# Softmax scores and gated-attention products as pairs of 64-row matmuls, with matmul operands at multiples of 128 bytes

## The chip, the cores and the metric

The kernel runs on one core of one Trainium2 chip. The metric is device time in microseconds (us) of one execution, the median of several runs.

## The reference, cut to what matters

One decoder layer on x of 2048 tokens by 1024 channels, float32. The normed input is projected by w_in to the inputs of three branches; their outputs are joined, scaled, projected by w_out and added to x; then comes a gated MLP with a short causal convolution.

```python
proj = rms(x) @ w_in                       # (2048, 2064)
# gated linear attention, 4 heads, dk 32, dv 64, chunks of 64 tokens
attn = where(causal, einsum('nid,njd->nij', q_dec, k_inv), 0)    # per chunk and head
o = attn @ v + q_dec @ state_before                              # per chunk and head
# sliding-window attention, 8 query heads of 64 on 2 key/value heads, blocks of 128
scores = q @ k_window.T * 64**-0.5 + band_bias                   # (128, 256) per head and block
out = softmax_with_sink(scores) @ v_window
# causal convolution of width 31, layer norm, silu; then
x = x + concat(o_a, o_b, o_c) * branch_scale @ w_out
x = x + (silu(gate) * val) @ w_down
```

## The kernel before, in words

All 2048 tokens are handled in four chunks of 512 (`NCH`, `T`), each of four blocks of 128 (`NT`, `P`). The program has three stages. The attention stage, up to 858 us, holds norm, input projection (`in_proj`, the groups gA to gD), the three branches (`attention`) and the output projection (`out_proj`; the last chunk's falls into the next pools and its tile is again called op). The two FFN stages (the u tiles up to 1705 us, then the d tiles) follow.

Products of accuracy are done in three: an operand is split into a high and a low part of type float32r (`split`, `piece_split`), and `mm3` (lines 145 to 148) issues high by high (L146), high by low (L147) and low by high (L148). Plain float32 matmuls (ga, gd, go) show as two matmul instructions each, as they go in two passes.

Events carry positions written out by hand (`SCHED`), and are emitted in that order; the framework then orders the instructions of each engine anew, by when it takes their inputs to be ready and by emission, and gives out buffers as they come free. So matmuls of different events stand between each other on TensorE (PE). PSUM has eight banks: four of pool A (`bankA`, accumulators of the projections) and four of pool B (`bankB`), which all transposes and all products of the branches share, one bank a tile.

The scores of one block are in `s2` of `swa_steps` (lines 687 to 724). Four transposes put the normed q into PSUM, `split` writes it to `qT` (ScalarE, ACT, the high part; VectorE, DVE, the low part). For each of four head pairs j, `mm3` multiplies qT, whose partitions hold the 64 channels of two heads, by `kz`. kz holds the keys of each of the two key heads in its own half of the partitions and zeros in the other, so that one 128-row matmul of 512 columns gives the scores of both heads (256 keys each) in one bank. In the first block of all only 128 keys exist and the matmul has 256 columns. Two reductions (L707) then add the bias and take the maximum. `k_norm_b` writes kz, one half of the partitions at a time (L551 on ACT, L552 on DVE).

The gated attention's inner products are in `g1` (lines 595 to 608): `qbd` holds the decayed q of four heads block-diagonally (four ACT copies of 32 rows), one float32 matmul ga (L604) of 128 rows and 512 columns gives all four heads' products in one bank, and L607 on DVE copies them under a mask to `attn`. In `g2`, L617 multiplies the two 64-token halves of `kts` and `va`: two matmuls of 64 rows, on partitions 0 to 63 and 64 to 127, into two banks (gd and go).

Addresses, in bytes within a partition, follow from the pools in order, every tile rounded up to 32 bytes, behind 16384 bytes of DMA scratch:

| tile | first address | past a multiple of 128 |
|---|---|---|
| mix, hT (attention), hb (FFN) | 18560, 34944, 51328, 67712 | 0 |
| kz | 95424 | 64 |
| vp | 105664 | 64 |
| wz | 92320 | 32 |
| hl (split weights, attention stage) | 125888, then every 4096 | 64 |
| qT, pT | 213536, 217888 | 32 |
| hl, hu (from 812 us on, FFN) | 174208, then every 4096 | 0 |
| hg, hw (second FFN stage) | 98432, 114816, then every 4096 | 0 |

Of the kernel before, what the change touches and what calls it, by code (L numbers as in the profile page):

```python
# [21 lines left out]
T = 512  # L22
NT = T // P
NCH = S // T
EPS = 1e-6
NEG = -1e30
# [15 lines left out]
NPRE = 4  # L42
OLD, OLA = 4, 1.5
NSC = NCH // 2
KH = KD // 2
# [20 lines left out]
def f32(ap):  # L66
    return ap.bitcast(F32)
# [3 lines left out]
def hymba_layer(  # L71
# [50 lines left out]
    def bankB(n):  # L122
        return psB.tile([P, T], F32, tag="b", name=n)
# [186 lines left out]
    cst = cp.tile([P, N_CST], F32, name="cst")  # L310
    tails = cp.tile([P, NUP, 2], F32, name="tails")
    with ExitStack() as p1:
        c1 = p1.enter_context(tc.tile_pool(name="c1", bufs=1))
        bt = c1.tile([P, SH, 2 * BLK], F32, name="bt")
        negsink = c1.tile([P, SH], F32, name="negsink")
        wz = c1.tile([P, KD, 32], F32R, name="wz")
        wa2 = c1.tile([32, P], F32, name="wa2")
# [3 lines left out]

        kz = c1.tile([P, 2, 2, (NT + 1) * BLK], F32R, name="kz")
        vp = c1.tile([P, NT + 1, 2, 192], F32R, name="vp")
        attn_b = c1.tile([P, GH, P], F32, name="attn")
        qbd = c1.tile([P, GH, P], F32, name="qbd")
        st_b = [c1.tile([P, GH * GDV], F32, name=f"st{i}") for i in range(2)]
# [4 lines left out]
        xp = p1.enter_context(tc.tile_pool(name="xp", bufs=2))  # L331
        ip = p1.enter_context(tc.tile_pool(name="ip", bufs=1))
        resp = p1.enter_context(tc.tile_pool(name="resp", bufs=2))
        at = p1.enter_context(tc.tile_pool(name="at", bufs=1))

        def tmp(n):
# [10 lines left out]

        for b in [f32(kz), f32(vp), attn_b, qbd, halo] + st_b:
            dve.memset(b, 0.0)
# [183 lines left out]
        def k_norm_a(c, t, a):  # L533
            sq = at.tile([P, P], F32, tag="ksq", name=f"ksq{c}_{t}")
            st = at.tile([P, 4], F32, tag="kst", name=f"kst{c}_{t}", bufs=2)
            act.activation(out=sq, in_=a[:, 0:P], func=AF.Square)
            dve.tensor_reduce(out=st[:, 0:2], in_=sq.rearrange("p (s d) -> p s d", d=SHD), axis=AX.X, op=ALU.add)
            rstd_of(st[:, 2:4], st[:, 0:2], 2, 1.0 / SHD)
            av = a[:, 0:P].rearrange("p (s d) -> p s d", d=SHD)
            pool.tensor_tensor(out=av, in0=av, in1=st[:, 2:4].unsqueeze(2).broadcast_to([P, 2, SHD]), op=ALU.mult)  # L540

        def k_norm_b(c, t, a):
            if t == 0 and c > 0:
                dve.tensor_copy(kz[:, :, :, 0:BLK], f32(kz[:, :, :, NT * BLK:]))
# [12 lines left out]
            split(dH, dL, vv)  # L557

        def gla_gates(c, d):
# [16 lines left out]
            e2 = at.tile([P, T], F32, tag="e2", name=f"e2_{c}")  # L576
            dec = at.tile([P, T // GC], F32, tag="dec", name=f"dec_{c}")
            qk = d["qk"]
# [12 lines left out]
        def gla_steps(c, d, mix):  # L591
# [3 lines left out]
            def g1(t):  # L595
                qd, ki, kt, dec = d["g"]
                ts = slice(t * P, (t + 1) * P)
                ap = bankB(f"ga{c}_{t}")
                for h in range(GH):
                    hs = slice(h * GDK, (h + 1) * GDK)  # L600
                    act.copy(qbd[hs, h, :], qd[hs, ts])
                dp = bankB(f"gd{c}_{t}")
                pe.transpose(dp[:, 256:256 + P], kt[:, ts], ident)
                pe.matmul(ap, ki[:, ts], qbd.rearrange("p h i -> p (h i)"), start=True, stop=True)  # L604
                kts = at.tile([P, P], F32, tag="kts", name=f"kts{c}_{t}")
                act.copy(kts, dp[:, 256:256 + P])
                dve.copy_predicated(attn_b.rearrange("p h i -> p (h i)"), gmask.rearrange("p h i -> p (h i)"), ap)  # L607
                w[t].update(dp=dp, kts=kts)

            def g2(t):  # L610
# [21 lines left out]
                sq = at.tile([P, 256], F32, tag="osq", name=f"osq{c}_{t}")  # L632
                ss = at.tile([P, 8], F32, tag="oss", name=f"oss{c}_{t}", bufs=2)
                act.activation(out=sq, in_=op[:, 0:256], func=AF.Square)
# [24 lines left out]
        def q_norm(c, t, q):  # L659
            sq = at.tile([P, T], F32, tag="tmp", name=f"qsq{c}_{t}", bufs=NTMP)  # L660
            st = at.tile([P, 16], F32, tag="qst", name=f"qst{c}_{t}", bufs=2)
# [11 lines left out]
        def swa_steps(c, t, d, mix):  # L673
# [13 lines left out]
            def s2():  # L687
                tp = bankB(f"qtp{c}_{t}")
                for j in range(4):
                    pe.transpose(tp[:, j * P:(j + 1) * P], w["qn"][:, j * P:(j + 1) * P], ident)  # L690
                qT = at.tile([P, 2, T], F32R, tag="qT", name=f"qT{c}_{t}")
                split(qT[:, 0, :], qT[:, 1, :], tp)
# [3 lines left out]
                else:  # L696
                    s_sb = [at.tile([P, 4, 2 * BLK], F32, tag=f"s{s}", name=f"s{s}_{c}_{t}") for s in range(2)]
                st = at.tile([P, 4, SH], F32, tag="sst", name=f"sst{c}_{t}", bufs=2)
                for j in range(4):
                    sp_ = bankB(f"sc{c}_{t}_{j}")  # L700
                    so = sp_[:, 0:2 * wd]
                    js = slice(j * P, (j + 1) * P)
                    ks = slice(t * BLK + o0, (t + 2) * BLK)
                    mm3(so, qT[:, 0, js], qT[:, 1, js], kz[:, 0, :, ks], kz[:, 1, :, ks], True, True)
                    for s in range(2):
                        h = 2 * j + s
                        dve.tensor_tensor_reduce(out=s_sb[s][:, j, o0:], in0=sp_[:, s * wd:(s + 1) * wd],  # L707
                                                 in1=bt[:, h, o0:], scale=1.0, scalar=NEG,
                                                 op0=ALU.add, op1=ALU.max, accum_out=st[:, 0, h:h + 1])
                dve.scalar_tensor_tensor(out=st[:, 0, :], in0=st[:, 0, :], scalar=-1.0, in1=negsink,  # L710
# [14 lines left out]
            def s3t(i):  # L725
                s, kb = combos[i]
                tp = bankB(f"ptp{c}_{t}_{s}{kb}")
                for j in range(4):
                    pe.transpose(tp[:, j * P:(j + 1) * P], w["sv"][s][:, j, kb * BLK:(kb + 1) * BLK], ident)
                pT = at.tile([P, 2, T], F32R, tag="pT", name=f"pT{c}_{t}_{s}{kb}", bufs=2)  # L730
                split(pT[:, 0, :], pT[:, 1, :], tp)
                w[i] = pT
# [26 lines left out]
        def conv_steps(c, d):  # L759
# [15 lines left out]
            def c1_(t):  # L775
                ts = slice(t * P, (t + 1) * P)
                tp = bankB(f"cy{c}_{t}")
                for i in range(2):
                    pe.transpose(tp[:, i * P:(i + 1) * P], ys[i][:, ts], ident)
                bn = at.tile([P, 12], F32, tag="bn", name=f"bn{c}_{t}", bufs=2)  # L780
# [585 lines left out]
```

## Time and profile before

| | |
|---|---|
| median of 3 runs (lowest, highest) | 2141.02 us (2140.99, 2143.72) |
| the profiled execution | 2137.3 us |
| its span, first to last instruction | 2135.6 us |
| PE busy | 2076.2 us |
| DVE busy | 1703.3 us |
| ACT busy | 1187.8 us |
| mean granted clock of TensorE | 0.994 |

The span is what the profile's rows add up to; the profiled execution's own time is 1.7 us longer. Busy time of PE counts a matmul from its start to its modelled end, and neighbouring matmuls overlap, so the rate of a stream is read from the distance between starts. PEld is the loading of weights, which runs beside the matmuls.

### The profile page before, as it was taken

The page shows a single profiled execution, that of the slowest core. Times are in us where ns is not written, and L with a number is a line of the kernel's source. Part 1 is how long each engine was busy: PE and PEld are TensorE (multiplying, and loading weights), DVE is VectorE, ACT ScalarE, POOL GpSimd, SP SyncE. Part 2 cuts the span into 40 slices and gives each one's busy share as a digit, 9 for nine tenths or more (in the row PEclk, how much of TensorE's full clock was granted, in tenths as well). Part 3 has the DMA queues.
Part 4 walks back from the last instruction along what each step waited for, and adds up shares of the span by engine and source line. Part 5 has one row for each costly group of instructions (what it writes and reads, how often), then busy time and mean ns, then how long its engine had stood idle before and what let it go on. Part 6 is the DMA issues. An engine that isn't in the chain of part 4 may idle for free.

```text
span 2135.6 us, 27892 instructions
## 1 busy us (share of the span) xinstructions
PE 2076.2 (97%) x9296; PEld 1658.3 (78%) x9296; DVE 1703.3 (80%) x2898; ACT 1187.8 (56%) x2281; POOL 295.4 (14%) x400
## 2 busy tenths in 40 slices
PE   6999999999999999999999999999999999999999
PEld 5766777777777767888888888888888868888887
DVE  4987986798689777877888978787787789678965
ACT  5467656766686665665655545455454534444443
POOL 1132121221121210011000013222122000000000
PEclk9999999999999999999999999999999999999999
DMA  4222224342433217544444576222222295887262
GB/s 141 86 91 63 60 86 147 94 119 93 135 103 101 66 59 245 175 132 147 152 165 168 182 260 218 79 71 98 79 89 79 89 346 161 290 281 232 70 207 89
DMA packets 183923, 296.22 MB, mean 139 GB/s; under 512 B 18832, under 2 KB 98019, under 8 KB 183779
## 3 DMA queue, kind: packets, MB, share of 16 engines
q1 hardware_dynamic: 183779, 294.45, 42.1%
q8 instruction: 73, 1.20, 0.2%
q14 instruction: 71, 0.58, 0.1%
HBM read 231.45 MB, written 62.93 MB: 138 GB/s over the span
## 4 chain that ended last, share of the span: by engine, by line
PE 78%; DVE 8%; ACT 6%; DMA 3%; issue 3%; POOL 2%; SPq 0%; ACTq 0%; DVEq 0%; POOLq 0%
PE uX L148 7%; PE uX L146 7%; PE uX L147 7%; PE dX L146 4%; PE dX L147 4%; PE dX L148 4%; PE uY L148 3%; PE uY L146 3%; PE uY L147 3%; PE op L146 3%; PE op L148 2%; PE op L147 2%; PE uZ L148 2%; PE uZ L146 2%; PE uZ L147 2%
## 5 line engine op out<-in xcount | busy, mean ns | idle before, releaser
L146 PE MATMUL uX<-hb,hu 128*128 128x512 f32 x704 | 274.2, 390 | 0.0
L148 PE MATMUL uX<-hb,hu 128*128 128x512 f32 x704 | 273.9, 389 | 0.0
L147 PE MATMUL uX<-hb,hu 128*128 128x512 f32 x704 | 273.9, 389 | 0.0
L1089 DVE SCALAR_TENSOR_TENSOR fy<-fu,fcw,fy 128x1024 f32<-128x1024 f32 x176 | 223.4, 1277 | 3.6 <-ACT fy L1087 3.3
L142 ACT ACTIVATE hu<-wu 128x512 fp32r<-128x512 f32 x132 | 82.5, 631 | 190.3 <-PE uX L148 73.0
L143 DVE TENSOR_TENSOR hu<-wu,hu 128x512 fp32r<-128x512 f32 x132 | 90.4, 688 | 105.2 <-ACT hu L142 105.1
L770 DVE SCALAR_TENSOR_TENSOR y<-u,cst,y 128x512 f32<-128x512 f32 x240 | 173.8, 753 | 0.1
L147 PEld LDWEIGHTS uX<-hb,hu 128*128 128x128 f32 x704 | 132.2, 188 | 27.4
L148 PEld LDWEIGHTS uX<-hb,hu 128*128 128x128 f32 x704 | 132.2, 188 | 27.4
L146 PEld LDWEIGHTS uX<-hb,hu 128*128 128x128 f32 x704 | 132.2, 188 | 27.2
L142 ACT ACTIVATE hu<-ws 128x512 fp32r<-128x512 f32 x176 | 108.1, 628 | 64.5 <-DVE ws L1011 48.8
L1060 POOL COPY fu<-tails 128x2 f32<-128x2 f32 x44 | 96.0, 2182 | 311.1 <-DVE fy L1089 307.5
L1087 ACT ACTIVATE fy<-fu,fcw 128x1024 f32<-128x1024 f32 x88 | 109.3, 1242 | 51.3 <-DVE fu L1011 37.6
L148 PE MATMUL uY<-hb,hu 128*128 128x512 f32 x352 | 136.9, 389 | 0.8 <-DVE hu L143 0.8
L146 PE MATMUL uY<-hb,hu 128*128 128x512 f32 x352 | 137.1, 389 | 0.0
L147 PE MATMUL uY<-hb,hu 128*128 128x512 f32 x352 | 136.9, 389 | 0.0
L146 PE MATMUL dX<-hw,hg 128*128 128x512 f32 x336 | 130.2, 389 | 1.0 <-ACT hg L142 1.0
L147 PE MATMUL dX<-hw,hg 128*128 128x512 f32 x336 | 130.7, 389 | 0.0
L148 PE MATMUL dX<-hw,hg 128*128 128x512 f32 x336 | 130.6, 389 | 0.0
L143 DVE TENSOR_TENSOR hu<-ws,hu 128x512 fp32r<-128x512 f32 x176 | 118.2, 683 | 10.4 <-ACT hu L142 10.4
L142 ACT ACTIVATE hg<-g 128x512 fp32r<-128x512 f32 x84 | 53.0, 632 | 126.4 <-PE dX L148 73.6
L146 PE MATMUL op<-hl_wo,mix 128*128 128x512 f32 x256 | 106.4, 420 | 2.1 <-ACT hl_wo L133 2.1
(320 smaller groups left out, 5387.0 us busy)
## 6 DMA issues: line engine op xcount, KB each, us to landing
wd<-in_w_down_dram SPq DMA_DIRECT2D x194, 256.0 KB
wu<-in_w_up_dram SPq DMA_DIRECT2D x176, 256.0 KB
g_d<-fy SPq DMA_DIRECT2D x44, 512.0 KB
g<-g_d SPq DMA_DIRECT2D x44, 512.0 KB
hb_d<-ho SPq DMA_DIRECT2D x28, 512.0 KB
hb<-hb_d SPq DMA_DIRECT2D x7, 2048.0 KB
st_gA<-in_w_in_dram SPq DMA_DIRECT2D x32, 256.0 KB
st_gB<-in_w_in_dram SPq DMA_DIRECT2D x64, 128.0 KB
```

Of the source, the lines that this page charges most:

```text
L142: act.activation(out=dst_h, in_=src, func=AF.Copy)
L143: dve.tensor_tensor(out=dst_l, in0=src, in1=f32(dst_h), op=ALU.subtract)
L146: pe.matmul(ps, aH, bH, start=first, stop=False, skip_group_check=go_on)
L147: pe.matmul(ps, aH, bL, start=False, stop=False, skip_group_check=go_on)
L148: pe.matmul(ps, aL, bH, start=False, stop=last, skip_group_check=go_on)
L770: dve.scalar_tensor_tensor(out=ys[i], in0=u[:, k:k + T], scalar=wc, in1=ys[i], op0=ALU.mult, op1=ALU.add)
L1060: pool.tensor_copy(u[:, 0:2], tails[:, ct, :])
L1087: act.activation(out=y, in_=u[:, 2:], func=AF.Identity, scale=cwt(2, ct), bias=cwt(3, ct))
L1089: dve.scalar_tensor_tensor(out=y, in0=u[:, w:w + 2 * T], scalar=cwt(w, ct), in1=y, op0=ALU.mult, op1=ALU.add)
```

## The change

1. The scores: kz loses its zero halves and has one column range for both key heads. Each 128-row matmul of 512 columns becomes two 64-row matmuls of 256 columns, on partitions 0 to 63 and 64 to 127, each into a bank of its own. Two head pairs share two banks.
2. ga becomes two such matmuls, two heads each, in two banks; qbd is half as wide, and the masked copy is done in two.
3. kz is written by one ACT and one DVE instruction for all 128 partitions, and is not zeroed at the start.
4. The tiles are put in another order, small ones go to a pool of their own (`sm`), qT and pT to another (`pqp`), and unused tiles (`cpad`, `c1pad`, `xpad`) fill gaps. The DMA scratch shrinks from 16384 to 4096 bytes. By the same sums, mix, hT and hb then start at 8192 and every 16384 behind it, kz at 73728, hl at 112640 (attention) and 163840 (later), qT at 129024; all these are multiples of 128, and the tiles of the FFN stages lie 10368 bytes (81 x 128) lower than before.

```diff
+CPAD = 480
+C1PAD = 816
...
+    cp.tile([P, CPAD], F32, name="cpad")
...
+        kz = c1.tile([P, 2, (NT + 1) * BLK], F32R, name="kz")
+        attn_b = c1.tile([P, GH, P], F32, name="attn")
+        vp = c1.tile([P, NT + 1, 2, 192], F32R, name="vp")
         bt = c1.tile([P, SH, 2 * BLK], F32, name="bt")
+        qbd = c1.tile([P, 2, P], F32, name="qbd")
...
-        kz = c1.tile([P, 2, 2, (NT + 1) * BLK], F32R, name="kz")
-        qbd = c1.tile([P, GH, P], F32, name="qbd")
...
+        c1.tile([P, C1PAD], F32, name="c1pad")
...
+        pqp = p1.enter_context(tc.tile_pool(name="pqp", bufs=1))
...
-        for b in [f32(kz), f32(vp), attn_b, qbd, halo] + st_b:
+        for b in [f32(vp), attn_b, qbd, halo] + st_b:
...
-            for s in range(2):
-                ps = slice(s * SHD, (s + 1) * SHD)
-                act.activation(out=kz[ps, 0, s, bs], in_=tp[ps, 0:P], func=AF.Copy, scale=kg[ps, :])
-                dve.scalar_tensor_tensor(out=kz[ps, 1, s, bs], in0=tp[ps, 0:P], scalar=kg[ps, :],
-                                         in1=f32(kz[ps, 0, s, bs]), op0=ALU.mult, op1=ALU.subtract)
+            act.activation(out=kz[:, 0, bs], in_=tp[:, 0:P], func=AF.Copy, scale=kg)
+            dve.scalar_tensor_tensor(out=kz[:, 1, bs], in0=tp[:, 0:P], scalar=kg, in1=f32(kz[:, 0, bs]),
+                                     op0=ALU.mult, op1=ALU.subtract)
...
-                ap = bankB(f"ga{c}_{t}")
+                ap = [bankB(f"ga{c}_{t}{i}") for i in range(2)]
                 for h in range(GH):
                     hs = slice(h * GDK, (h + 1) * GDK)
-                    act.copy(qbd[hs, h, :], qd[hs, ts])
+                    act.copy(qbd[hs, h % 2, :], qd[hs, ts])
...
-                pe.matmul(ap, ki[:, ts], qbd.rearrange("p h i -> p (h i)"), start=True, stop=True)
+                for i in range(2):
+                    ps = slice(i * 2 * GDK, (i + 1) * 2 * GDK)
+                    pe.matmul(ap[i][:, 0:2 * P], ki[ps, ts], qbd[ps].rearrange("p h i -> p (h i)"), start=True, stop=True)
...
-                for j in range(4):
-                    sp_ = bankB(f"sc{c}_{t}_{j}")
-                    so = sp_[:, 0:2 * wd]
-                    js = slice(j * P, (j + 1) * P)
-                    ks = slice(t * BLK + o0, (t + 2) * BLK)
-                    mm3(so, qT[:, 0, js], qT[:, 1, js], kz[:, 0, :, ks], kz[:, 1, :, ks], True, True)
+                ks = slice(t * BLK + o0, (t + 2) * BLK)
+                for jp in range(2):
+                    sb = [bankB(f"sc{c}_{t}_{jp}{s}") for s in range(2)]
+                    for j in (2 * jp, 2 * jp + 1):
+                        js = slice(j * P, (j + 1) * P)
+                        os_ = slice((j % 2) * wd, (j % 2 + 1) * wd)
+                        for a, b in ((0, 0), (0, 1), (1, 0)):
+                            for s in range(2):
+                                ps = slice(s * SHD, (s + 1) * SHD)
+                                pe.matmul(sb[s][:, os_], qT[ps, a, js], kz[ps, b, ks], start=(a == 0 and b == 0),
+                                          stop=(a == 1))
...
-    nc = _bacc.Bacc("TRN2", target_bir_lowering=False, num_devices=1)
+    nc = _bacc.Bacc("TRN2", target_bir_lowering=False, num_devices=1, dynamic_dma_scratch_size=4096)
```

## Rows read from the trace of the kernel before

**Rows 1.** Busy time, share of span, instructions of PE and PEld, of the page.

```profile
PE 2076.2 (97%) x9296; PEld 1658.3 (78%) x9296; DVE 1703.3 (80%) x2898; ACT 1187.8 (56%) x2281; POOL 295.4 (14%) x400
```

**Rows 2.** Stretches: us; busy of PE, PEld, DVE, ACT, POOL; clock, DMA share, GB/s.

```profile
0.00:858.00 858.00, 807.05 (x3687) 612.66 (x3688) 678.26 (x1454) 545.12 (x1282) 167.32 (x256) 0.99 0.35 106
858.00:1705.00 847.00, 846.17 (x3765) 700.99 (x3764) 685.05 (x901) 462.53 (x692) 128.09 (x144) 1.00 0.40 136
```

**Rows 3.** Timeline of PE (start, us, instruction): first and last rows of four streams.

```profile
56.30 0.40 PE L146 MATMUL ip_gB<-hT,hl_gB 128*128 128x512 f32 x1
...
67.28 0.39 PE L148 MATMUL ip_gB<-hT,hl_gB 128*128 128x512 f32 x1
...
275.31 0.39 PE L147 MATMUL ip_gD<-hl_gD,hT 128*128 128x512 f32 x1
...
287.91 0.39 PE L148 MATMUL ip_gD<-hl_gD,hT 128*128 128x512 f32 x1
...
816.61 0.40 PE L147 MATMUL op<-hl_wo,mix 128*128 128x512 f32 x1
...
858.13 0.39 PE L148 MATMUL op<-hl_wo,mix 128*128 128x512 f32 x1
...
1661.17 0.39 PE L146 MATMUL uX<-hb,hu 128*128 128x512 f32 x1
...
1671.82 0.39 PE L148 MATMUL uX<-hb,hu 128*128 128x512 f32 x1
```

**Rows 4.** Timeline of PE: score matmuls, first and last rows of two streams.

```profile
420.78 0.40 PE L147 MATMUL sc<-kz,qT 128*128 128x512 f32 x1
...
423.12 0.39 PE L148 MATMUL sc<-kz,qT 128*128 128x512 f32 x1
...
156.12 0.29 PE L146 MATMUL sc<-kz,qT 128*128 128x256 f32 x1
...
156.72 0.28 PE L148 MATMUL sc<-kz,qT 128*128 128x256 f32 x1
```

**Rows 5.** Timeline of PE around a pair of L617, between two op matmuls.

```profile
325.88 0.40 PE L148 MATMUL op<-hl_wo,mix 128*128 128x512 f32 x1
326.20 0.48 PE L617 MATMUL gd<-va,kts 64*128 64x256 f32 x1
326.21 0.48 PE L617 MATMUL go<-va,kts 64*128 64x256 f32 x1
326.52 0.38 PE L617 MATMUL gd<-va,kts 64*128 64x256 f32 x1
...
326.83 0.50 PE L146 MATMUL op<-hl_wo,mix 128*128 128x512 f32 x1
327.17 0.40 PE L147 MATMUL op<-hl_wo,mix 128*128 128x512 f32 x1
```

**Rows 6.** Timeline of PE: one half of L617 alone, and what follows it.

```profile
370.04 0.70 PE L617 MATMUL go<-va,kts 64*128 64x256 f32 x2
370.67 0.88 PE L619 MATMUL go<-va,attn 128*128 128x64 f32 x6
```

**Rows 7.** Timeline of PE: the two passes of ga, and what follows them.

```profile
340.53 1.02 PE L604 MATMUL ga<-qbd,e 128*128 128x512 f32 x2
341.39 0.60 PE L729 MATMUL ptp<-ident,s 128*128 128x128 f32 x4
```

**Rows 8.** Timeline of PE: first rows of the three runs of one block's scores.

```profile
364.44 0.42 PE L146 MATMUL sc<-kz,qT 128*128 128x512 f32 x1
...
367.30 0.72 PE L148 MATMUL sc<-kz,qT 128*128 128x512 f32 x2 [0.27 <-DVE qT L143]
...
369.03 0.39 PE L146 MATMUL sc<-kz,qT 128*128 128x512 f32 x1
```

**Rows 9.** Groups of DVE: instruction, shapes, count; busy us, mean ns; idle before.

```profile
L607 DVE COPY_PREDICATED attn<-gmask,ga 128x512 f32<-128x512 uint8 x16 | 11.7, 734 | 1.0 <-PE ga L604 0.9
...
L552 DVE SCALAR_TENSOR_TENSOR kz<-ktp,kg,kz 64x128 fp32r<-64x128 f32 x32 | 11.1, 348 | 3.1 <-ACT kz L551 2.6
```

More of the change, by code (lines that the diff above doesn't have):

```diff
@@ L311, in hymba_layer @@
     tails = cp.tile([P, NUP, 2], F32, name="tails")
+    cp.tile([P, CPAD], F32, name="cpad")
     with ExitStack() as p1:
         c1 = p1.enter_context(tc.tile_pool(name="c1", bufs=1))
+        kz = c1.tile([P, 2, (NT + 1) * BLK], F32R, name="kz")
+        attn_b = c1.tile([P, GH, P], F32, name="attn")
+        vp = c1.tile([P, NT + 1, 2, 192], F32R, name="vp")
         bt = c1.tile([P, SH, 2 * BLK], F32, name="bt")
+        qbd = c1.tile([P, 2, P], F32, name="qbd")
+        st_b = [c1.tile([P, GH * GDV], F32, name=f"st{i}") for i in range(2)]
+        wz = c1.tile([P, KD, 32], F32R, name="wz")
         negsink = c1.tile([P, SH], F32, name="negsink")
-        wz = c1.tile([P, KD, 32], F32R, name="wz")
         wa2 = c1.tile([32, P], F32, name="wa2")
@@ L320, in hymba_layer @@
         smask = c1.tile([P, 256], F32, name="smask")
-        kz = c1.tile([P, 2, 2, (NT + 1) * BLK], F32R, name="kz")
-        vp = c1.tile([P, NT + 1, 2, 192], F32R, name="vp")
-        attn_b = c1.tile([P, GH, P], F32, name="attn")
-        qbd = c1.tile([P, GH, P], F32, name="qbd")
-        st_b = [c1.tile([P, GH * GDV], F32, name=f"st{i}") for i in range(2)]
         halo = c1.tile([P, 2, CW - 1], F32, name="halo")
+        c1.tile([P, C1PAD], F32, name="c1pad")
         wp["st"] = p1.enter_context(tc.tile_pool(name="wst", bufs=3))
         wp["hl"] = p1.enter_context(tc.tile_pool(name="whl", bufs=4))
+        pqp = p1.enter_context(tc.tile_pool(name="pqp", bufs=1))
         xp = p1.enter_context(tc.tile_pool(name="xp", bufs=2))
+        xp.tile([P, 16], F32, tag="xpad", name="xpad", bufs=1)
         ip = p1.enter_context(tc.tile_pool(name="ip", bufs=1))
@@ L534, in k_norm_a @@
             sq = at.tile([P, P], F32, tag="ksq", name=f"ksq{c}_{t}")
-            st = at.tile([P, 4], F32, tag="kst", name=f"kst{c}_{t}", bufs=2)
+            st = sm.tile([P, 4], F32, tag="kst", name=f"kst{c}_{t}", bufs=2)
             act.activation(out=sq, in_=a[:, 0:P], func=AF.Square)
@@ L576, in gla_gates @@
             e2 = at.tile([P, T], F32, tag="e2", name=f"e2_{c}")
-            dec = at.tile([P, T // GC], F32, tag="dec", name=f"dec_{c}")
+            dec = sm.tile([P, T // GC], F32, tag="dec", name=f"dec_{c}")
             qk = d["qk"]
@@ L660, in q_norm @@
             sq = at.tile([P, T], F32, tag="tmp", name=f"qsq{c}_{t}", bufs=NTMP)
-            st = at.tile([P, 16], F32, tag="qst", name=f"qst{c}_{t}", bufs=2)
+            st = sm.tile([P, 16], F32, tag="qst", name=f"qst{c}_{t}", bufs=2)
             act.activation(out=sq, in_=q, func=AF.Square)
@@ L690, in s2 @@
                     pe.transpose(tp[:, j * P:(j + 1) * P], w["qn"][:, j * P:(j + 1) * P], ident)
-                qT = at.tile([P, 2, T], F32R, tag="qT", name=f"qT{c}_{t}")
+                qT = pqp.tile([P, 2, T], F32R, tag="qT", name=f"qT{c}_{t}")
                 split(qT[:, 0, :], qT[:, 1, :], tp)
@@ L697, in s2 @@
                     s_sb = [at.tile([P, 4, 2 * BLK], F32, tag=f"s{s}", name=f"s{s}_{c}_{t}") for s in range(2)]
-                st = at.tile([P, 4, SH], F32, tag="sst", name=f"sst{c}_{t}", bufs=2)
-                for j in range(4):
-                    sp_ = bankB(f"sc{c}_{t}_{j}")
-                    so = sp_[:, 0:2 * wd]
-                    js = slice(j * P, (j + 1) * P)
-                    ks = slice(t * BLK + o0, (t + 2) * BLK)
-                    mm3(so, qT[:, 0, js], qT[:, 1, js], kz[:, 0, :, ks], kz[:, 1, :, ks], True, True)
[L705 to L709, printed above, removed]
+                st = sm.tile([P, 4, SH], F32, tag="sst", name=f"sst{c}_{t}", bufs=2)
+                ks = slice(t * BLK + o0, (t + 2) * BLK)
[9 more added lines that the diff above has]
+                                          stop=(a == 1))
+                        for s in range(2):
+                            h = 2 * j + s
+                            dve.tensor_tensor_reduce(out=s_sb[s][:, j, o0:], in0=sb[s][:, os_],
+                                                     in1=bt[:, h, o0:], scale=1.0, scalar=NEG,
+                                                     op0=ALU.add, op1=ALU.max, accum_out=st[:, 0, h:h + 1])
                 dve.scalar_tensor_tensor(out=st[:, 0, :], in0=st[:, 0, :], scalar=-1.0, in1=negsink,
@@ L779, in c1_ @@
                     pe.transpose(tp[:, i * P:(i + 1) * P], ys[i][:, ts], ident)
-                bn = at.tile([P, 12], F32, tag="bn", name=f"bn{c}_{t}", bufs=2)
+                bn = sm.tile([P, 12], F32, tag="bn", name=f"bn{c}_{t}", bufs=2)
                 dve.bn_stats(bn[:, 0:6], tp[:, 0:256])
```

12 lines of the change are left out of this document (8 added, 4 removed).

## The prediction

> **What bounds the kernel now.** I read the page's busy table first: TensorE is busy for 97% of the span [rows 1]. The table by stretches then says where that is not the whole story. In the attention stage, up to 858 us, PE is busy for 807 of 858 us; in the first FFN stage for 846 of 847 [rows 2]. So a matmul's nanoseconds are the program's time, nearly one for one, and what counts is the distance between the starts of neighbouring matmuls, not the duration shown for one (about 390 ns, which overlaps the next). The timeline gives that distance. Four unbroken streams of 128x512 matmuls, each given by its first and last row: ip_gB goes from 56.30 to 67.28 in 47 steps, 233.5 ns each; ip_gD from 275.31 to 287.91 in 55 steps, 229.1 ns; op from 816.61 to 858.13 in 183 steps, 226.9 ns; uX from 1661.17 to 1671.82 in 47 steps, 226.7 ns [rows 3]. All are the same operation at the full granted clock. What differs is the address of the split weights: hl lies 64 bytes past a multiple of 128 in the attention stage and is the weight operand in ip_gB, the moving one in ip_gD; from 812 us on, op takes it from a pool at a multiple of 128, as uX does. The scores, with qT 32 and kz 64 bytes past, go at 234 ns (420.78 to 423.12, 10 steps) [rows 4].
>
> **Alignment.** The change puts hl, kz, qT, pT, vp and wz at multiples of 128 and moves all later tiles by 81x128, so the FFN stages keep their place modulo 128. The gain per matmul, to 226.7: 6.7 ns where hl is the weight (768 of ip_gA and ip_gB), 5.1 us; for 768 of ip_gC and ip_gD 229.1 gives 2.4 ns, but in places the same stream steps by 233, so I take 3.2 ns, 2.5 us; the same for 576 of op, 1.9 us; for 186 of so, both operands off, the scores' 7 ns, 1.3 us; 64 of z at most 0.4 us. Together 11 us if PE always sets the pace, nothing if the addresses are not the cause. As PE is idle for 6% of this stage and waits stay where another engine ends them, I take 9.5 us.
>
> **A page against it.** The Trainium skill (SBUF — State Buffer, Door 1) says that SBUF has lines of 16 bytes and that contiguous reads within them go at full bandwidth. By it a start at 32 or 64 is as good as one at 128, and this term would be 0. The two op and ip_gD streams speak against that [rows 3].
>
> **Scores, the streams.** One score step of a head pair is now a full-array matmul against a kz that is zero in the other half. The new one is two 64-row matmuls of 256 columns. The trace has a pair of this shape already, L617: its halves (two instructions each, as fp32 goes in two passes) start 0.01 us apart and take 0.63 us from the first start to the next operation's, 326.20 to 326.83 [rows 5]. A half that stands alone takes the same 0.63, from 370.04 to 370.67 [rows 6]. So the second half is free when it directly follows the first. A 256-column score matmul of the full array, own weight load included, goes at 0.12 us (156.12 to 156.72, 5 steps) [rows 4]; I price the new pair at that. Against 234 ns it saves 116 ns, for 12 steps in each of 15 blocks 20.9 us. The first block already has 256 columns and gains nothing I count.
>
> **Scores, the visits.** Halves and full array do not follow each other freely. From op at 325.88 to op at 327.17 is 1.29 us [rows 5]. Two op matmuls take 0.46 of it and two passes of 256 columns 0.43 (half of the two passes of 512 in ga, 0.86 us from 340.53 to 341.39 [rows 7]). So one visit to the 64-row mode costs 0.40 us beside its work. How many visits there are is decided by the framework's scheduler, which orders instructions by readiness and fills PE's waits with other matmuls. In the trace the 16 blocks' score matmuls stand in 32 separate runs; one block runs as 4, 5 and 3, from 364.44, 367.30 and 369.03, with projection matmuls between [rows 8]. With 32 visits the bill is 12.8 us, which leaves 8 us of gain. Where a run starts after a wait for the split of qT the entry is hidden, so the bill is a little less.
>
> **Scores, the banks.** A pair needs two PSUM banks at once out of four, and a torn pair saves nothing: six single halves take 0.71 us more than six pairs. In 9 of 16 blocks of the trace the last three matmuls stand apart, as at 369.03 [rows 8], because a fourth bank came late. If all nine tear there, 6.4 us are lost and the score gain is 1.6 us. Ends: 20.9 us gained with no visit charged; with every pair torn and 48 visits, 19 us lost. I take 4 us gained, between the whole and the half-torn sum.
>
> **Gated attention.** ga now costs 0.86 us [rows 7]. The pair costs 0.43 of work and a visit of 0.40, so 0.83: whole pairs gain 0.03 x 16 = 0.5 us. Torn, the second half pays another visit and its own 0.43: 0.83 more. L617, which also needs two banks, stands whole in only 7 of 16 cases, in 25 runs. If the same 9 tear, 7.5 us are lost. But the two ga banks are asked for together, right behind each other, while one of L617's belongs to the next tile; I take 2 us lost.
>
> **DVE, ACT and the rest.** Writing kz by one instruction in place of two drops 16 DVE instructions of 348 ns and as many of ACT's. The masked copy of 734 ns becomes two of half the width [rows 9]; the added time lies between nothing and a whole second copy, 16 x 0.73 = 12 us of DVE, and as the elements stay the same I take 2 us, near the lower end. Neither engine bounds this stage; if DVE's cover is gone, the 5.6 us dropped pay for it. The memset of kz is shorter, under the load of x. No DMA, store or queue order is edited; the smaller scratch serves none of these SP transfers. Where pairs stand behind a wait for the low half of qT, DVE comes last, as now.
>
> **Sum.** The profiled execution took 2137.3 us (span 2135.6 and 1.7 around it). 2137.3 - 9.5 - 4 + 2 = 2125.8. The median of the runs, 2141.0, lies 3.7 above that execution; on it the forecast is 2129.5. About 0.2%, 4.3 us, is what a measurement of this kernel can tell from no change.
>
> **Rivals.**
> - Pairs whole, few visits: alignment 9.5, scores 12 to 15, ga 0.5; 2116 to 2119. For it, qT is ready for both halves at once, and many runs start after a wait. Against it, 32 runs now. Chance 0.20.
> - Torn pairs, slower: the four banks of the B pool hand out one at a time, so the scheduler sends one half alone and fills in full-array work. 48 visits x 0.40 less nothing saved is +19, ga +7.5, alignment -9.5: about 2158. For it, rows 6 and 8; against it, it needs nearly all pairs torn. It decides from the point where visits and torn halves cost over 9.5 us more than the streams save. Chance 0.15. The Trainium skill (TensorEngine Tiling (Array Packing), Gotcha 1: PSUM Pressure) also says that row tiles need different banks and so more of them; no row shows the new demand.
> - Alignment is not the cause: other engines' traffic makes the 3 to 7 ns, and the change doesn't do there what it says. Then -4 + 2, 2139. For it, the attention stage has other work beside it; against it, ip_gD and the late op stream differ only there and in the address. Chance 0.10.
> - Loads do not hide in a half: each weight load waits until that half's matmul is through, some 0.11 us, so a pair takes 0.22 and streams save 2 us in place of 20.9: with 12.8 for visits the scores lose 11, sum 2144.5. Against it, the second pass in L617 starts 0.32 us after the first [rows 5], with 0.21 of it work; an unhidden second load would follow that, not stand within it. Chance 0.07. The Trainium skill (TensorE: Matmul & The Clock Gate, Part 3, The mechanism) has such a rule: loads overlap a running matmul only when the row groups differ. By that rule 2144.5; the trace does not agree.
>
> **How the numbers follow.** The forecast as summed, from 2120 to 2138, has 0.48. Faster by over 0.2%: 0.41 of it, 0.20 and 0.03, so 0.64. Slower: 0.13 of the torn case and 0.03 of the loads, so 0.16. Same: 0.20. One in ten below 2111 (whole pairs, almost no visits) and one above 2146 make the range; order changes over the whole stage can move waits by some us either way and are within it.
>
> **What would show it.** In the profile after, ip_gB steps at about 227 ns and uX still at 226.7; score matmuls read 64x256, their halves 0.01 us apart, pair to pair 0.12; few full-array matmuls between first and last of a block; idle PE before the scores by DVE qT unchanged. Wrong would be: streams still at 233; halves of one step far apart with projection matmuls between; a uX step other than 226.7, since modulo 256 the FFN tiles do move; or a longer stretch of PE waits for ga's or the scores' banks.

## The result and the profile after

The changed kernel takes 2165.77 us (median of 5 runs, 2164.72 to 2169.92), against 2141.02 before (5 runs, 2136.89 to 2143.72): a ratio of 1.0118, 95% interval 1.0101 to 1.0134. It is slower by some 25 us. The forecast of 2129.5 has the wrong sign, and the range ends 20 us short. The profiled execution took 2165.83 us, 0.06 from the median; its busy line, beside [rows 1], is:

```profile
PE 2096.6 (97%) x9520; PEld 1665.3 (77%) x9520; DVE 1699.4 (79%) x2897; ACT 1182.0 (55%) x2265; POOL 293.1 (14%) x400
```

TensorE has 224 instructions more (192 for the scores, 32 for ga) and 20 us more of busy time. Where the time went shows in the stretches. In the kernel before, the first up-product (uX) starts at 858.36 us; now it starts at 887.79. So the table by stretches (us; busy of PE, PEld, DVE, ACT, POOL; granted clock, DMA share, GB/s) is cut at 888:

```profile
0.00:888.00 888.00, 828.28 (x3913) 620.04 (x3914) 672.61 (x1454) 539.83 (x1269) 163.71 (x256) 0.97 0.33 104
888.00:1733.00 845.00, 845.00 (x3760) 700.10 (x3759) 686.14 (x901) 461.67 (x689) 129.43 (x144) 1.00 0.40 135
```

The first FFN stage takes 845 us as before [rows 2], and the second as long as before. All of the loss, 29.4 us between the two profiled executions, lies in the attention stage. The mean clock there is 0.97 where it was 0.99 [rows 2].

The streams did speed up. First and last rows of one ip_gB stream and one uX stream after, on PE's timeline (start, duration, instruction):

```profile
223.77 0.39 PE L148 MATMUL ip_gB<-hT,hl_gB 128*128 128x512 f32 x1
...
231.70 0.39 PE L150 MATMUL ip_gB<-hT,hl_gB 128*128 128x512 f32 x1
...
922.19 0.39 PE L148 MATMUL uX<-hb,hu 128*128 128x512 f32 x1
...
932.85 0.39 PE L150 MATMUL uX<-hb,hu 128*128 128x512 f32 x1
```

35 steps of ip_gB take 7.93 us, 226.6 ns each, against 233.5 [rows 3]; uX goes at 226.7 in 47 steps, as before. So the loss stands elsewhere, and one block of scores shows it. PE's timeline of the block at 243 us; "x6" are six 64-row products in a row, and what stands between them are projection matmuls of 128 rows:

```profile
243.22 0.39 PE L149 MATMUL ip_gC<-hl_gC,hT 128*128 128x512 f32 x1
243.54 0.74 PE L718 MATMUL sc<-kz,qT 64*128 64x256 f32 x6
244.21 0.50 PE L150 MATMUL ip_gC<-hl_gC,hT 128*128 128x512 f32 x1
244.54 0.39 PE L148 MATMUL ip_gC<-hl_gC,hT 128*128 128x512 f32 x1
...
245.10 0.74 PE L718 MATMUL sc<-kz,qT 64*128 64x256 f32 x6
245.77 0.50 PE L150 MATMUL ip_gC<-hl_gC,hT 128*128 128x512 f32 x1
246.20 1.12 PE L718 MATMUL sc<-kz,qT 64*128 64x256 f32 x9
247.24 0.50 PE L148 MATMUL ip_gC<-hl_gC,hT 128*128 128x512 f32 x1
...
248.05 0.40 PE L148 MATMUL ip_gC<-hl_gC,hT 128*128 128x512 f32 x1
248.37 0.61 PE L718 MATMUL sc<-kz,qT 64*128 64x256 f32 x3
248.92 0.49 PE L149 MATMUL ip_gC<-hl_gC,hT 128*128 128x512 f32 x1
```

The block's 24 products stand in four runs of 6, 6, 9 and 3. The step before a run is 0.32 us instead of 0.23 (243.22 to 243.54), the step behind it 0.33 (244.21 to 244.54). In the whole trace there are 67 such runs, where the scores of the kernel before stood in 32. In the program's order only 100 of 192 pairs of halves stand whole, and 184 halves are single. VectorE in the same block:

```profile
243.90 0.69 DVE L145 TENSOR_TENSOR qT<-qtp,qT 128x512 fp32r<-128x512 f32 x1
...
245.52 0.42 DVE L722 CUSTOM_DVE_ANT_0 s<-sc,bt 128x256 f32<-128x256 f32 x1 [0.27 <-PE sc L718]
...
245.87 0.42 DVE L722 CUSTOM_DVE_ANT_0 s<-sc,bt 128x256 f32<-128x256 f32 x1
...
247.89 0.42 DVE L722 CUSTOM_DVE_ANT_0 s<-sc,bt 128x256 f32<-128x256 f32 x1
```

Reductions follow each other at 0.35 us (245.52, 245.87), so the two of a head pair take 0.70 us, while its three product pairs need three times 0.115. The odd head pair writes the second half of the bank that the even pair's reduction is reading, and the program lets it start only behind that reduction: the last run, at 248.37, starts when the reduction of 247.89 is through (0.42 later, 248.31). The view of the tile sc lists for what the engines sat idle at its instructions (us, times), weight loads (PEld) and matmuls (PE) together; after:

```profile
  PE sc L718: 18.0, 30
  DVE sst L722: 13.3, 29
  ACT qT L144: 8.4, 16
  DVE qT L145: 5.2, 7
```

The second line, waits for a reduction, is not in the same list of the kernel before. Asked for by engine (PEld first, then PE), it is

```profile
  DVE sst L722: 10.5, 25
  DVE sst L722: 2.8, 4
```

So most of it is idle time of the weight loads, while matmuls still run; the matmuls themselves stood idle for 2.8 us of it. What the waits do to the order weighs more, as the run with grouped reductions shows below. The first line is VectorE waiting for products; before, it was

```profile
  PE sc L148: 3.1, 11
```

At half clock (1.2 GHz) TensorE spends 47.8 us of the attention stage instead of 23.9. One of the new stretches, beside the block's scores at 279 to 287 us:

```profile
279.00:282.00 3.00, 1.46 (x11) 0.89 (x10) 3.00 (x6) 0.52 (x2) 1.67 (x2) 1.00 0.53 165
282.00:285.00 3.00, 3.00 (x17) 2.19 (x17) 2.71 (x13) 0.00 (x0) 0.00 (x0) 0.89 0.30 87
285.00:288.00 3.00, 3.00 (x9) 1.87 (x8) 1.31 (x4) 0.72 (x1) 0.00 (x0) 0.50 0.00 0
```

PE is busy for 1.46 of 3 us, waiting for qT, before the granted clock falls to 0.50; VectorE is busy all of the 3.

### The profile page after: what moved, and what is told of

It is laid out like the page before. It is cut to its first block, busy times and chain, and to the rows that moved or that the text cites. A ratio compares the mean times of both kernels' runs of the same rounds, so it can differ in the third digit from the quotient of the medians.

```text
span 2164.1 us, 28290 instructions
## 1 busy us (share of the span) xinstructions
PE 2096.6 (97%) x9520; PEld 1665.3 (77%) x9520; DVE 1699.4 (79%) x2897; ACT 1182.0 (55%) x2265; POOL 293.1 (14%) x400
## 4 chain that ended last, share of the span: by engine, by line
PE 82%; DVE 6%; ACT 5%; DMA 2%; issue 2%; POOL 2%; SPq 0%; DVEq 0%; ACTq 0%; POOLq 0%
PE uX L149 7%; PE uX L148 7%; PE uX L150 7%; PE uY L148 4%; PE uY L150 4%; PE uY L149 4%; PE dX L148 3%; PE dX L149 3%; PE dX L150 3%; PE op L150 3%; PE op L148 3%; PE op L149 3%; PE sc L718 2%; PE uZ L149 2%; PE uZ L148 2%
## 5 line engine op out<-in xcount | busy, mean ns | idle before, releaser
L1102 ACT ACTIVATE fy<-fu,fcw 128x1024 f32<-128x1024 f32 x88 | 109.3, 1242 | 47.8 <-DVE fu L1026 35.1
```

The lines of the kernel that those rows point to most:

```text
L1102: act.activation(out=y, in_=u[:, 2:], func=AF.Identity, scale=cwt(2, ct), bias=cwt(3, ct))
```

## The experiments

The kernel before took 2138.9 to 2140.4 us (medians) beside these runs; each ratio is to it. "Runs" below are runs of score products on TensorE's timeline.

**Which part loses.** The addresses alone, with scores, kz and ga as before:

```
-C1PAD = 816
+C1PAD = 16
...
+        kz = c1.tile([P, 2, 2, (NT + 1) * BLK], F32R, name="kz")
...
+                    mm3(so, qT[:, 0, js], qT[:, 1, js], kz[:, 0, :, ks], kz[:, 1, :, ks], True, True)
```

> Addresses alone: the new order of tiles, pads and pools, with the scores, kz and ga as they were before (full-array matmuls). Theory A (the torn 64-row pairs make the loss): no 64-row score visit, so it runs faster than the kernel before by what the steps of ip_gA, ip_gB and so show in the profile after (234 to 229 ns, some 950 matmuls), about 5 us: 2136. Theory C (the new addresses or the new order of the small tiles are the loss): slower than before, 2150 to 2165.

Measured: 2142.72, ratio 1.0018 (1.0010 to 1.0027). A miss: the addresses gained nothing. The steps of the attention stage's projections are 232 to 233 ns, though every operand lies at a multiple of 128.

The same with the changed ga:

```
-                ap = bankB(f"ga{c}_{t}")
+                ap = [bankB(f"ga{c}_{t}{i}") for i in range(2)]
```

> Addresses and ga as pairs, scores as before. Theory A: the loss sits in the scores, so this lies near the addresses alone plus what ga's pairs cost: 16 blocks, two or three torn, at most 6 us, 2136 to 2143. Rival (ga's three banks in place of two starve the other users of pool B): 2150 or more.

Measured: 2148.61, ratio 1.0048 (1.0036 to 1.0060), 5.9 us above the run before it. That is above theory A's range, as the addresses had gained nothing, and at the end of the 6 us that it gave the ga pairs.

The changed kernel with ga as before:

```
-                ap = [bankB(f"ga{c}_{t}{i}") for i in range(2)]
+                ap = bankB(f"ga{c}_{t}")
```

> Addresses and scores as pairs, ga as before. Theory A: nearly all of the loss stays, 2158 to 2164. Rival (ga's banks): it falls back to about the kernel before, 2140 or less.

Measured: 2164.01, ratio 1.0113 (1.0097 to 1.0129). As expected: nearly the whole loss is in the scores.

**Why the score pairs lose.** The products of two head pairs ahead of their four reductions, so that no product waits for a reduction in its own bank:

```
                     for j in (2 * jp, 2 * jp + 1):
...
                                           stop=(a == 1))
+                    for j in (2 * jp, 2 * jp + 1):
+                        os_ = slice((j % 2) * wd, (j % 2 + 1) * wd)
                         for s in range(2):
                             h = 2 * j + s
```

> The changed kernel, but the products of two head pairs are issued before their four reductions, so no product waits for a reduction that reads the same bank. Theory A (that order tears the pairs): more pairs whole and about a quarter fewer visits to the 64-row mode; 25 visits less at 0.40 us and some 47 pairs more at 0.115 us, about 15 us faster than the changed kernel: 2150. Rival B (a visit costs what it costs, and the tearing comes from banks that are late): as slow as the changed kernel, 2160 to 2170.

Measured: 2151.69, ratio 1.0061 (1.0048 to 1.0073), 12 to 14 us below the changed kernel (by the ratios, by the medians). 40 runs are left of 67, and the wait for a reduction is nearly gone from the list of the tile sc:

```profile
  DVE sst L724: 1.1, 3
```

The same with ga as before:

> The run with the grouped reductions (2151.7), and ga as before in one product of 128 rows: 38 runs of score products instead of 67, none of ga. Theory A: the ga pairs cost 6 us there as they did beside the old scores (2148.6 against 2142.7), so 2144 to 2148. Rival (the ga pairs cost only what they cost in the run with paired scores alone, 2164.0 against 2165.8): 2149 to 2152.

Measured: 2148.29, ratio 1.0031 (1.0021 to 1.0041). At the upper end of the first range, though the ga pairs are worth only 3.4 us here.

Then the changed order of scores, banks and reductions, with all 128 rows and the zero half of kz in each product:

```
-                                ps = slice(s * SHD, (s + 1) * SHD)
-                                pe.matmul(sb[s][:, os_], qT[ps, a, js], kz[ps, b, ks], start=(a == 0 and b == 0),
+                                pe.matmul(sb[s][:, os_], qT[:, a, js], kz[:, b, s, ks], start=(a == 0 and b == 0),
```

> The changed kernel's scores in everything (two heads in two banks, two head pairs in one bank one after the other, the same reductions in the same places, 24 products of 256 columns per block), but each product with all 128 rows and the zero half of kz as before; inner products ga as before; addresses as in the changed kernel. Against the run with paired scores alone (2164.0) only the 64-row mode is gone. Theory A (each run of 64-row products costs an entry and an exit, and the order of reductions and products in one bank makes 67 runs of 32): without the mode the torn order costs almost nothing, 2132 to 2140. Rival B (products of the odd head pair that wait for a reduction, and work that comes late behind them, cost the time whatever the rows are): 2155 to 2164.

Measured: 2142.44, ratio 1.0009 (0.9999 to 1.0019). Some 2 us above the range of theory A, 13 below that of the rival. The same torn order, in 65 runs, costs 3.8 us with full rows (above the 2138.6 of the next paragraph) and 25.4 with 64-row products. Its timeline of the block at 242 us:

```profile
241.71 0.52 PE L714 MATMUL sc<-kz,qT 128*128 128x256 f32 x3
242.06 0.40 PE L149 MATMUL ip_gC<-hl_gC,hT 128*128 128x512 f32 x1
242.30 0.40 PE L150 MATMUL ip_gC<-hl_gC,hT 128*128 128x512 f32 x1
242.53 1.58 PE L714 MATMUL sc<-kz,qT 128*128 128x256 f32 x12
```

Steps between score and projection matmuls are plain steps here (241.71 to 242.06 are three products of 0.117 us, 242.30 to 242.53 one step of 0.23): a tear costs nothing. Waits for reductions are 3.2 us in 8 places in the list of the tile sc here, and 16.4 us in 32 with paired scores alone.

**Which addresses matter.** One pad more, so that a weight pair and the activations start at the same place modulo 2048:

```
-C1PAD = 16
+C1PAD = 304
```

> The addresses alone again, as in the run that expected 2136 and took 2142.7, but with one pad of 1152 bytes more per partition, so that a weight pair (hl) starts at the same place modulo 2048 bytes as the activations it is multiplied with (both 0), where that run had 896 against 0. Theory P (the relative place of the two operands of a 512-column matmul sets its step, not the multiple of 128): steps of the projections about 229 ns as in the changed kernel, against 232.4 in that run; some 3000 of them before the first up-product give 10 us back: 2130 to 2135. Rival (the changed order of the tensors, not the place, cost that run its gain): steps and time stay at 232 ns and about 2142.

> The same with 128 bytes of pad more than the run that took 2142.7: hl at 1024 modulo 2048, activations at 0. Theory P with a period of 2048 bytes: steps stay near 232 ns, 2142. With a period of 1024 bytes or a divisor of it: steps near 229 ns, 2130 to 2135.

> The addresses alone, with hl at 1536 modulo 2048 bytes and the activations at 0 (so far: 896 gave steps of 232.4 ns, 0 and 1024 gave 228.5). If the place modulo 512 or less sets the step: about 228.5 ns, 2136 to 2140; if modulo 1024: about 232.4, 2141 to 2144.

> The same with hl at 1280 modulo 2048. If the place modulo 256 sets the step: about 228.5 ns, 2136 to 2140; if modulo 512 or 1024: about 232.4, 2141 to 2144.

| hl against hT, modulo 2048 | mean step of ip_gA, ip_gB | time | ratio (interval) |
|---|---|---|---|
| 832 (before: 960 and 128) | 233.3 ns | | |
| 896 (the first run above) | 232.5 | 2142.72 | 1.0018 (1.0010 to 1.0027) |
| 0 | 228.6 | 2138.61 | 0.9991 (0.9982 to 1.0000) |
| 1024 | 228.4 | 2137.89 | 0.9988 (0.9979 to 0.9997) |
| 1536 | 228.6 | 2136.89 | 0.9984 (0.9974 to 0.9995) |
| 1280 | 228.5 | 2137.34 | 0.9985 (0.9972 to 0.9998) |

The steps fell as theory P said, the time by less than half of what it said (2130 to 2135 in the first two); the last two lie in their quick ranges. A stream of ip_gB in the first run above (hl at 896):

```profile
203.38 0.40 PE L148 MATMUL ip_gB<-hT,hl_gB 128*128 128x512 f32 x1
...
211.75 0.40 PE L150 MATMUL ip_gB<-hT,hl_gB 128*128 128x512 f32 x1
```

and in the run with hl at 0:

```profile
203.11 0.39 PE L148 MATMUL ip_gB<-hT,hl_gB 128*128 128x512 f32 x1
...
211.27 0.39 PE L150 MATMUL ip_gB<-hT,hl_gB 128*128 128x512 f32 x1
```

36 steps each: 8.37 us, 232.5 ns, and 8.16 us, 226.7 ns. Of the places tried, those that differ by a multiple of 256 bytes are quick, and 128 short of one is slow. In these runs only hl moved, with hT at 0; that the difference counts, and not hl's own place, is shown by uX: hb and hu both lie 128 past a multiple of 256 before and at one after, and it goes at 226.7 ns in both.

**Pairs in whole visits.** Grouped reductions, old ga, and of the three terms the one with the low part of q first, which comes last from VectorE. Then everything is there when the first product may start:

```
-                        for a, b in ((0, 0), (0, 1), (1, 0)):
+                        for a, b in ((1, 0), (0, 0), (0, 1)):
```

> The run with grouped reductions and old ga (2148.3), and of the three terms of a product the one with the low part of q first: no score product can start before the low part of q is there, and then all that it needs is there, so the framework's order has 20 runs of score products instead of 38, 12 of 16 blocks whole in one visit, 169 pairs with 46 single halves instead of 153 with 78. Theory A (runs of 64-row products are what the time goes into): from the run with full rows and the same addresses (2138.6), pairs 169 and singles 46 at 0.115 us against 384 half-length products at 0.117 give -20, 20 runs at 0.40 give +8: 2127, 2123 to 2133, faster than both kernels. Rival D (the 64-row products cost something beside the runs' ends, in the clock for instance, which lay low in the stage between 24 and 75 us in the runs so far): 2138 to 2146.

Measured: 2146.75, ratio 1.0026 (1.0014 to 1.0038). A miss by 14 to 24 us; rival D's range holds it. And yet the visits are as designed. PE's timeline of the block at 242 us:

```profile
242.02 0.39 PE L149 MATMUL ip_gC<-hl_gC,hT 128*128 128x512 f32 x1
242.34 1.69 PE L713 MATMUL sc<-kz,qT 64*128 64x256 f32 x24
243.96 0.50 PE L150 MATMUL ip_gC<-hl_gC,hT 128*128 128x512 f32 x1
244.29 0.40 PE L148 MATMUL ip_gC<-hl_gC,hT 128*128 128x512 f32 x1
```

From 242.02 to 244.29 are 2.27 us; less two projection steps (0.46), the block takes 1.81 us: 12 pairs of 0.115 and 0.43 for the visit. As 12 full-row steps of 0.234 [rows 4] it takes 2.81. VectorE begins the first reduction at 243.93, behind three operations of the convolution, and needs 0.35 us for each of eight:

```profile
241.94 2.06 DVE L782 SCALAR_TENSOR_TENSOR y<-u,cst,y 128x512 f32<-128x512 f32 x3
243.93 0.42 DVE L719 CUSTOM_DVE_ANT_0 s<-sc,bt 128x256 f32<-128x256 f32 x1
...
246.34 0.42 DVE L719 CUSTOM_DVE_ANT_0 s<-sc,bt 128x256 f32<-128x256 f32 x1
```

So the softmax gets its last maximum no sooner than VectorE can deliver it. The time that TensorE saved comes back further on, as waits for ACT and VectorE, which come late to the copies of q and the splits of pT behind the softmax:

```profile
293.43 0.50 PE L148 MATMUL op<-hl_wo,mix 128*128 128x512 f32 x1 [0.98 <-ACT q L513]
...
295.88 0.51 PE L148 MATMUL so<-pT,vp 128*128 128x512 f32 x1 [1.26 <-ACT pT L144]
...
298.98 0.80 PE L149 MATMUL so<-pT,vp 128*128 128x512 f32 x1 [1.68 <-DVE pT L145]
```

The table by stretches there:

```profile
292.00:296.00 4.00, 1.75 (x10) 0.99 (x7) 3.45 (x6) 4.00 (x10) 1.11 (x4) 1.00 0.35 103
296.00:300.00 4.00, 2.32 (x9) 1.62 (x10) 2.37 (x4) 2.06 (x4) 1.60 (x1) 0.78 0.00 0
300.00:304.00 4.00, 4.00 (x13) 3.22 (x12) 2.53 (x5) 1.71 (x3) 0.00 (x0) 0.50 0.42 131
```

and the same of the run with full rows and hl at 0:

```profile
292.00:296.00 4.00, 4.00 (x22) 3.38 (x21) 3.75 (x7) 3.55 (x7) 2.60 (x2) 1.00 0.22 65
296.00:300.00 4.00, 4.00 (x19) 3.10 (x19) 2.69 (x6) 1.86 (x4) 1.87 (x3) 1.00 0.18 66
300.00:304.00 4.00, 4.00 (x18) 2.96 (x17) 3.77 (x7) 2.15 (x7) 2.80 (x3) 1.00 0.19 55
```

With whole visits PE loses 3.9 of 8 us to waits and then goes at half clock; with full rows it has work in all 12. (In the whole attention stage the clock is halved for 51.2 us in the one, 30.7 in the other.)

> The changed kernel with the two edits (grouped reductions, low part of q first) and its ga pairs: 20 runs of score products, 19 of ga. Theory A: the run beside it with the old ga plus the price of the ga pairs (5.9, 3.4 and 1.8 us in the three comparisons so far): 2129 to 2133. Rival D: 2142 to 2150.

Measured: 2150.12, ratio 1.0045 (1.0029 to 1.0061): the changed kernel with both repairs, at the upper end of rival D's range. The ga pairs cost 3.4 us once more.

The control, the order of the terms alone:

> A control: the kernel with new addresses, full-row scores and old ga (2138.6), and only the order of the three terms changed, low part of q first (17 runs of score products instead of 32). Theory A: without 64-row products the number of runs costs nothing, 2137 to 2140. If the order of the terms gives by itself what the run with pairs gains: 2127 to 2133.

Measured: 2142.47, ratio 1.0018 (1.0006 to 1.0029). That is above theory A's range too: the order by itself gains nothing and costs 4 to 6 us. So about half of the 8 us by which whole visits lie above full rows belongs to the order. Beside full rows in the same order they lie 4.3 us above by medians, 2.3 by means, give or take 2.6: about level.

And the low part first alone, reductions between the products:

> The run with paired scores alone (2164.0, 67 runs of score products) with the low part of q first and nothing else: the reductions stay between the products of two head pairs, 45 runs. Theory A (the ends of the runs): between 2148.3 (38 runs) and 2164.0, by their number 2150 to 2154. Rival H (what grouping gave was the later place of the reductions on VectorE, not the fewer runs): 2160 to 2164.

Measured: 2161.47 (4 runs, 2155.9 to 2163.17, the profiled one the fastest), ratio 1.0096 (1.0076 to 1.0116). A miss: by the number of runs it should have been 2150 to 2154, and rival H's range holds it. 45 runs are left, but the list of the tile sc has as many waits for reductions as with paired scores alone (16.4 us, 32 times there; 3.4 us of it on the matmuls themselves in both):

```profile
  DVE sst L717: 15.2, 34
```

So the 15.7 us that grouping gave (2164.0 to 2148.3) do not go by the number of runs alone. How much ending the waits gave is not shown: 22 runs fewer at 0.40 us would be 9 us, against 2.5 measured by medians, and with 4 and 5 runs, which spread over 7 and 13 us, the two cannot be told apart.

**VectorE relieved.** Every second tap of the convolution left out:

```
-                    for n in range(lo, hi)]
+                    for n in range(lo, hi) if n // 2 % 2 == 0]
```

> The kernel with new addresses, full-row scores and old ga (2138.6), with every second of the 31 taps of the convolution left out (30 of 62 operations of 0.75 us on VectorE in each of four chunks, 90 us of its work; the convolution's result is then another). The reference for the next two. If VectorE holds the attention stage up only at its waits: the 56 us of PE waits and 31 us at half clock of that run shrink by a part, 2100 to 2125.

> The run with grouped reductions and low part first (2146.75, that is 8 us above full rows), with the same taps left out. Theory E (the visits do save TensorE time, 767 to 760 us of its steps outside waits and low clock, but VectorE, busy 4.0 of every 4 us from 276 to 292 us, ends no sooner, so TensorE runs out of work, waits for pT and falls to half clock): with VectorE relieved the pairs are worth their saving, 5 to 13 us below the run beside it. Rival F (64-row products bring waits and low clock with them whatever VectorE does): still 4 to 10 us above it.

> The changed kernel with the same taps left out: 65 runs of score products, 18 of ga. Theory A and E: its visits cost TensorE 30 us of steps themselves, which no relief of VectorE gives back: 18 to 30 us above the run with full rows and half the taps. Rival G (the changed kernel lost by VectorE's waits): within 10 us of it.

Measured: 2137.15, 2134.94 and 2159.25, ratios 0.9989 (0.9980 to 0.9999), 0.9983 (0.9973 to 0.9992) and 1.0104 (1.0087 to 1.0122). VectorE's busy time falls by some 76 us (from 1704.1 to 1627.5 with full rows), as neighbouring taps overlap. Full rows gain 1.5 us by it, which is within the noise and misses the expected 2100 to 2125; whole visits gain 11.8. So whole visits go from 8 us above full rows to 2 below, by means 2.1, give or take 2.0. That is theory E's direction, though less than its 5 to 13, and not rival F. The changed kernel stays 22 us above full rows, as theories A and E said. Full rows in whole visits' order of terms were not run with half the taps.

## Why the prediction was wrong

The steps, in the prediction's order.

**Alignment: right stream, wrong condition, too large.** ip_gB does go at 226.7 ns where it was 233.5. But the multiple of 128 is not what does it: at a multiple of 128 that is 896 off, it goes at 232.5. And 226.7 is what an unbroken stream reaches; over the stage the mean is 229. ip_gC, ip_gD and op went at 230 already; the first two gained 1.5 ns and op 0.4, where 3.2 was taken. By these steps some 6 us were to be had, and as time 1.4 to 3.5 us came (2140.0 to 2138.6, and 2140.4 to 2136.9), where the sum had 9.5. The page cited against this term, the Trainium skill (SBUF — State Buffer, Door 1), has lines of 16 bytes and by them no gain from any of these places; the streams at 226.7 and 232.5 ns disagree.

**Scores, the streams: right.** Pairs step by 0.115 us where 0.12 was taken. The rival in which loads do not hide falls with it. The Trainium skill (TensorE: Matmul & The Clock Gate, Part 3, The mechanism) lets a load overlap a running matmul only when the row groups differ; the trace does not agree. In the run at 248.37, three products of one half, the weight loads start at 248.37, 248.48 and 248.60, and the first product runs until 248.76.

**Scores, the visits: the price right, the number wrong. This is the step that failed.** A whole visit measured 0.43, the price taken was 0.40. The number was read off the kernel before, 32 runs, as if the new instructions would be torn in the same places. There are 67, and 92 of the 192 pairs are torn.

**Scores, the banks: the wrong cause.** Tears were looked for where a bank comes late. They come, by the run with grouped reductions, from a wait inside a bank: two head pairs share one, and the reduction of the first stands between. The step on VectorE ("neither engine bounds this stage") looked at the whole stage; at this place the pair's products shrink to 0.35 us while its two reductions stay at 0.70, so VectorE becomes the slower one. With full rows, 0.70 against 0.70, the same order has 65 runs too; so the number comes from the order, and the cost from the 64-row visits, as without them the tears cost next to nothing. How much the slower reductions add to it was not separated.

The size of it: the runs of scores, each from the start of the matmul before it to the start of the one behind it, sum to 60.7 us before and 84.6 after. Less one projection step of 0.23 per run, plus 0.11 for the longer step behind each 64-row run, that is 53.4 and 76.6: 23 us lost where the sum had 4 gained. At the prediction's own prices, 20.9 us are saved, 67 visits cost 26.8 and 92 torn pairs 10.6, so 16.5 us are lost. The other 7 are about what the half clock adds: 7 of the 67 runs, 12.9 us of the 84.6, lie in it.

**Gated attention: right in size in the changed kernel.** +2 was taken, and it measured 1.8 there, a difference within the noise of its 5 runs; 3.4, 3.4 and 5.9 us in three other comparisons, 5.9 where the scores are as before. A whole pair takes 0.63 us and 0.20 of longer steps around it, 0.83, as priced; 2 of the 16 were torn in the changed kernel, not 9. What makes up the 5.9 was not looked into.

**The rival "torn pairs, slower"** came nearest, 2158 at a chance of 0.15: many visits, and much of the saving lost. It was held back by a condition (banks handed out one at a time) that was not the one that decides.

**A step that the prediction did not have: what the saved time is worth.** "A matmul's nanoseconds are the program's time, nearly one for one" holds for tears, not for savings. The scores' runs, worked out as above, against the time, both as differences to the run with full rows and hl at 0 (51.7 us, median 2138.6, profiled 2136.6; 54.4 us, 2137.15 and 2137.15 for the last line, with half the taps). The runs of scores are read from the profiled execution, so the rest, time less scores' runs, is taken to its time; the median stands beside it, and the two differ by as much as 11 us:

| kernel | runs | scores' runs | time, median | time, profiled | rest |
|---|---|---|---|---|---|
| full rows in the changed order | 65 | +6.6 | +3.8 | +9.5 | +3 |
| full rows, low part first | 17 | -0.5 | +3.9 | +5.9 | +6 |
| paired scores alone | 67 | +24.8 | +25.4 | +36.1 | +11 |
| grouped, old ga | 38 | +2.1 | +9.7 | +12.6 | +11 |
| grouped, low part first | 20 | -12.3 | +8.1 | +11.4 | +24 |
| the last, half the taps | 20 | -13.3 | -2.2 | 0.0 | +13 |

What is lost at the scores is lost in full. What is saved there comes back as waits and half clock, 24 us in the best case (20 by the median), 13 of which (11) are left when VectorE has some 76 us less to do. Some 6 (4) of the 24 come with the order of the terms, with full rows too. That VectorE's chain is a part of this is shown by the last two lines and by the run with half the taps and full rows, which gained 1.5. What makes up the rest was not settled: the waits for ACT are candidates, and whether 64-row work itself takes part in the falls of the clock was not tried apart from the waits beside it. No version with paired scores and all of the work beat the kernel before; full rows with the addresses in place did, by 0.1 to 0.2%, which is at the edge of what can be told.

## What to carry to other kernels

When a change shortens one engine's work at a place, set it against the other engine's work on the same data there, step by step (0.35 us of products against 0.70 of reductions), and not against a share of busy time over the stage. When an instruction form has a price for entering and leaving, don't read the number of visits from the old order: write the new order of writes and reads of each bank down, and put what reads a bank behind everything that fills it. And before a saving on the busiest engine is counted in full, look for the work that is to fill the time saved.

## What the runs showed of the hardware

The place of a float32r weight pair against the activations it meets sets the step of a 128x512 matmul: 226.7 ns in a stream with both at the same place modulo 2048, and means of 228.4 to 228.6 over a stage where their starts differ by a multiple of 256 bytes (0, 1024, 1280 and 1536 tried), 232.5 at 896 and 233.3 at 832, all at full clock. That both were multiples of 128 did not help at 896. This is with the weight pair as the weight operand; as the moving one (ip_gC, ip_gD) it went at 230 at 832, 232 to 233 at 896 and 228 to 229 at multiples of 256.

A visit of 64-row products among 128-row matmuls costs 0.40 us beside its work in L617 [rows 5] and 0.43 with 24 score products; the step into it is 0.32 us and the one behind it 0.33, where plain steps are 0.23. Products of 128 rows and 256 columns pay nothing at the same places.
